# Three buffers for converted weights, a Gram product for the first norm, and seven banks for one projection, in a fused two-block network

## The chip, the cores and the metric

The kernel runs on one core of a Trainium2 chip. The metric is the device time of one launch in microseconds. A core has five engines with their own instruction queues: TensorE (PE), VectorE (DVE), ScalarE (ACT), GpSimd (POOL) and SyncE (SP), which issues transfers. Data lies in HBM, in SBUF (128 partitions) and in PSUM, whose eight banks take PE's sums.

## The reference, cut to what matters

One sequence of 512 tokens of width 1024 passes through a first block and then through two hybrid layers (gqa, mLSTM, neighbourhood and differential attention, gated up projections, an FFN). The first block:

```python
xn = rmsnorm(x, norm1_w[l])
p = xn @ w_in[l]
z, xbc, dt_raw, p_rwkv, p_hgrn, p_gate = jnp.split(p, in_splits, axis=-1)
y_ssm = ssd_branch(z, xbc, dt_raw, ...) @ w_branch_ssm[l]
y_rwkv = rwkv7_branch(p_rwkv, ...) @ w_branch_rwkv[l]
y_hgrn = hgrn2_branch(p_hgrn, ...) @ w_branch_hgrn[l]
gates = jax.nn.sigmoid(p_gate).reshape(b, L, N_BRANCH, D_MODEL)
mixed = gates[:, :, 0] * y_ssm + gates[:, :, 1] * y_rwkv + gates[:, :, 2] * y_hgrn
x = x + mixed @ w_out[l]
h_gate, h_up = jnp.split(rmsnorm(x, norm2_w[l]) @ ffn_w_in[l], 2, axis=-1)
x = x + (jax.nn.silu(h_gate) * h_up) @ ffn_w_down[l]
```

`rmsnorm` divides by the root of the mean square over the 1024 channels; `ssd_branch` ends in such a norm too. All of it is f32.

## The kernel before, in words

Activations lie with channels on partitions and tokens along the row, as tiles of 128x512. A product of f32 quality is made of three f16 products: operands are split into a high and a low part, and xh·whi, xl·whi and xh·wlo are summed in PSUM (L1181 to L1183 in `fm_g`; L1216 to L1218 where the weight is the moving side).

**Weights.** They stream from HBM in units of 128x1024 (512 KB). `_emit_unit` puts one into a staging tile (`wst` for the foreground stream, `bst` for the background stream, two buffers each), ScalarE makes the high part (`whi`/`bhi`, L1070) and VectorE the low part (`wlo`/`blo`, L1071). Every second background unit of the early stages goes another way (L1065 to L1067, with GpSimd). One plain unit feeds 24 products. `take` hands out the next unit and, ahead of that, converts as many further units as `_room` allows: with two buffers per tag, one unit in use and one to come. `self.tags` counts the buffers that are taken.

**The FFN** (`ffn`, once per block or layer, 22 pairs of gate and up tiles) has, for every third pair, a product in seven parts of half width instead of eight ("sevenths", `seventh`, L1424 to L1426), whose weights are sums of quarters: `_emit_seventh` forms them with VectorE (`bw`, L1106, L1110), splits them (L1119 ScalarE or its mirror, L1120 VectorE) and puts them into whichever of the four weight tags is least used. Between products VectorE combines partial sums and scales them (L1440), GpSimd multiplies gate and up (POOL, L1440), and ScalarE and VectorE split the result into `hh` and `hl` (L1231, L1235). PE's outputs turn over five `acc` banks and two background banks bg0 and bg1 (`bank`).

**The first block.** `start` loads x (eight tiles), splits it into xh and xl, and calls `square_sums` for each: ScalarE squares (L1248), VectorE adds (L1250, into `sqa`), and PE sums over partitions by products with a column of ones (L1254). `rms` and `rows_of` turn the sums into a row `rb` over tokens (L1307 to L1309). After that the recurrent scans run, mixed with gates and projections that wait for no scan. At the end the state space branch (`ssd`) gives ysh and ysl and its own norm row `rbs`, and `up` makes the three up projections wbr, wbh and wbs in background mode: for each of eight outputs it loads a gate (`ug`, two buffers), for wbs multiplies it by rbs (L1336), lets PE make 24 products into bg0 or bg1 in turn, multiplies (L1341, L1343) and adds into `mg` on GpSimd (L1345). `out_ffn` then splits mg into mh and ml for the output projection wo1, whose every unit needs all eight.

**Order.** The program is written out by Python generators; a scheduler of the tile framework then sets each engine's order and its waits, so a change of one buffer count shifts rows through the whole program.

Of the kernel before, what the change touches and what calls it, by code (L numbers as in the profile page):

```python
# [11 lines left out]
F16 = mybir.dt.float16  # L12
# [13 lines left out]
PS = 1024.0  # L26
EPS = 1e-6
UB = 8
H = T // 2
FF7 = tuple(range(1, NF, 3))  # L30

# [203 lines left out]
class First:  # L235
# [686 lines left out]
    def first(self, next_gain):  # L922
        parts = lambda p, n, k: (self.t(p, [128, k, T], n + "h", F16), self.t(p, [128, k, T], n + "l", F16))
        pool = self.tc.tile_pool
        if True:
            gd = self.t(self.dram, [24, 128, T], "gd", bufs=1)
            yd = self.t(self.dram, [2, 2, 128, 4, T], "yd", F16, 1)
            with self.banks(acc=1, S=2, T=1, O=1, H=1), pool(name="f_rwkv", bufs=1) as mid, pool(name="f_rwkvs", bufs=2) as small:
                self.mid, self.small = mid, small
                gates, hgrn, due = self.gates("w1", 14, 24, gd), self.hgrn(yd[1]), [0.0, 0.0]  # L930

                def beside(g, h):
                    for n, (more, lane) in enumerate(((gates, 1), (hgrn, 0))):
                        due[n] += (g, h)[n]
                        self.lane, self.bgmode = lane, n == 1
                        while due[n] >= 1:
                            due[n] -= 1
                            next(more, None)
                    self.lane, self.bgmode = None, False

                self.rwkv(yd[0], beside)
                beside(1000, 1000)
            with ExitStack() as mgs:
                mp = mgs.enter_context(pool(name="f_mg", bufs=1))
                self.mg = self.t(mp, [128, 8, T], "mg")
                self.keep2 = self.upp = mp
                ysm = parts(mp, "ys", 8)
                yr, yg = parts(mp, "yr", 4), parts(mp, "yg", 4)
                with self.banks(acc=1, S=2, T=1, O=2), pool(name="f_ssd", bufs=1) as mid, pool(name="f_ssds", bufs=2) as small:
                    self.mid, self.small = mid, small  # L950
                    rbs = self.ssd(*ysm)
                    for y, d in ((yr, yd[0]), (yg, yd[1])):
                        for n in range(2):
                            self.nc.sync.dma_start(out=y[n], in_=d[n])
                    self.background(
                        self.up(gd, 1, "wbr", *yr, 4, True),
                        self.up(gd, 2, "wbh", *yg, 4),
                        self.up(gd, 0, "wbs", *ysm, 8, False, rbs),
                    )
                self.spare = False  # L960
                self.out_ffn(mgs, "wo1", "n2_f", "wf1", "wd1", "fin1", "x", next_gain, ("win0", 46))


class Net(First):
    def __init__(self, ctx, tc, io, cols_at, rows_at, order=None):
# [31 lines left out]
        self.known = order is not None  # L997
        self.emitted, self.taken, self.ready = [0, 0], [0, 0], {}
        self.bgmode, self.dense, self.spare, self.turn = False, False, True, 0
        self.lane, self.other = None, 1  # L1000


    def nm(self, s):
# [43 lines left out]
    def bank(self):  # L1047

        self.turn += 1
        n = self.nb["acc"]  # L1050
        if self.lane is not None or self.bgmode or (self.dense and self.turn % (n + 2) >= n):
            self.other = 1 - self.other if self.lane is None else self.lane
            return self.t(self.bgp, [128, T], f"bg{self.other}", bufs=1)
        return self.b("acc")


    def _emit_unit(self, s, name, u):
# [1 line left out]
        tag = "wb"[s]  # L1059
        st = self.t(self.wst, [128, UB, 128], tag + "st", F32, 2)  # L1060
        nc.sync.dma_start(out=st, in_=self.io[name][u])
        hi = self.t(self.wsp, [128, UB, 128], tag + "hi", F16, 2)
        lo = self.t(self.wsp, [128, UB, 128], tag + "lo", F16, 2)
        if s and self.spare and self.emitted[1] % 2:
            nc.scalar.activation(out=st, in_=st, func=AF.Copy, scale=WS)  # L1065
            nc.scalar.copy(out=hi, in_=st)
# [25 lines left out]
    def _emit_seventh(self, e, name, u, m):  # L1092
# [20 lines left out]
        if m == 6:  # L1113
            del self.staged[name, u]
        tag = min(("bhi", "blo", "whi", "wlo"), key=lambda t: self.tags[t])
        o = self.t(self.wsp, [128, 2, 4, 128], tag, F16, 2)
        self.tags[tag] += 1
        hi, lo = o[:, 0, 0:n], o[:, 1, 0:n]
        nc.scalar.activation(out=hi, in_=src, func=AF.Copy, scale=WS)  # L1119
# [3 lines left out]
    def _room(self, s, e, i):  # L1123
# [3 lines left out]
            return True  # L1127
        if s:
            at = lambda n: n[-1] if n[:2] == "wi" or n[:3] == "wup" else "f"
            return e < i + 2 and at(name) == at(self.items[s][i][0])  # L1130
        if m is None:
            plain = sum(k is None for _, _, k in self.items[s][i:e + 1])
            return plain < 3 and all(self.tags[t] < 2 for t in ("whi", "wlo"))
        return self.opened and min(self.tags.values()) < 2

    def take(self, name, u, m=None):
        s = int(self.bgmode)
# [132 lines left out]
    def rms(self, n, scale, within=None):  # L1270
# [3 lines left out]
        nc.vector.tensor_reduce(out=s, in_=self.ssq[:, 8 * n:8 * n + 8].rearrange("p (t k) -> p t k", k=2), axis=AX.X, op=ALU.add)  # L1274
        if within is not None:
            nc.vector.tensor_tensor(out=s, in0=s, in1=within, op=ALU.mult)
        f = 1.0 / (scale * scale)
        nc.vector.tensor_scalar(out=s, in0=s, scalar1=f / D, scalar2=f * EPS, op0=ALU.mult, op1=ALU.add)
        r = self.t(self.norms, [128, 4], f"rt{n}")
# [106 lines left out]
    def start(self, gain):  # L1386
        nc = self.nc
        with self.banks(acc=5, T=1), self.tc.tile_pool(name="x_in", bufs=1) as p:
            self.sqp = p
            x = self.t(p, [128, 8, T], "x")  # L1390
            for k in range(0, 8, 2):
                (nc.sync if k % 4 else nc.scalar).dma_start(out=x[:, k:k + 2], in_=self.xd[:, k:k + 2])
            for k in range(8):
                self.norm_tile(k, x[:, k], gain)
            self.norm_end()

    def out_ffn(self, mg, wout, gain2, wff, wdn, gain, last=False, after=None, then=None):

# [764 lines left out]
```

## Time and profile before

| | before |
|---|---|
| median of 3 runs | 3617.13 us (3607.03 to 3620.99) |
| profiled execution | 3613.31 us |
| its span, first to last instruction | 3611.6 us |
| mean granted PE clock | 0.976 |
| PE busy | 3338.2 us, 92% |
| VectorE busy | 2760.1 us, 76% |
| ScalarE busy | 1608.3 us, 45% |
| GpSimd busy | 752.6 us, 21% |

Stages by the profile's time: scans to about 680 us, the state space branch and the up projections to 1010, the first FFN's products from about 1080 to 1440, a hybrid layer to 2130, its FFN to 2540, the second layer to 3200, its FFN to the end. A wait that the profile puts beside a PE instruction is time in which PE stood idle just before it, with what ended that time.

### The profile page before, as it was taken

The page shows a single profiled execution, that of the slowest core. Times are in us where ns is not written, and L with a number is a line of the kernel's source. Part 1 is how long each engine was busy: PE and PEld are TensorE (multiplying, and loading weights), DVE is VectorE, ACT ScalarE, POOL GpSimd, SP SyncE. Part 2 cuts the span into 40 slices and gives each one's busy share as a digit, 9 for nine tenths or more (in the row PEclk, how much of TensorE's full clock was granted, in tenths as well). Part 3 has the DMA queues.
Part 4 walks back from the last instruction along what each step waited for, and adds up shares of the span by engine and source line. Part 5 has one row for each costly group of instructions (what it writes and reads, how often), then busy time and mean ns, then how long its engine had stood idle before and what let it go on. Part 6 is the DMA issues. An engine that isn't in the chain of part 4 may idle for free. (4 is left out here: it accounts for less than half of the span.)

```text
span 3611.6 us, 60781 instructions
## 1 busy us (share of the span) xinstructions
PE 3338.2 (92%) x23758; PEld 2033.9 (56%) x23758; DVE 2760.1 (76%) x5599; ACT 1608.3 (45%) x3009; POOL 752.6 (21%) x782
## 2 busy tenths in 40 slices
PE   7899999899899999999989999999999989999998
PEld 3565566555455577556545545568655545545567
DVE  6877777587777798788767677788788767777788
ACT  4232333255344344464556543344364455534443
POOL 2222223223332211201221132211201120132211
PEclk9999999899899999999999999999999999999999
DMA  4312213233242234323223353335322323363333
GB/s 141 82 57 59 75 49 91 72 126 114 88 164 94 94 106 146 106 63 96 93 82 109 116 159 96 96 112 159 111 65 80 94 90 100 112 185 110 94 100 94
DMA packets 151156, 368.16 MB, mean 102 GB/s; under 512 B 44098, under 2 KB 47428, under 8 KB 150868
## 3 DMA queue, kind: packets, MB, share of 16 engines
q1 hardware_dynamic: 117492, 336.03, 30.0%
q0 software_dynamic: 7680, 23.00, 1.9%
q10 hardware_dynamic: 25696, 5.25, 0.8%
q8 instruction: 186, 3.05, 0.4%
q14 instruction: 102, 0.84, 0.1%
HBM read 322.72 MB, written 40.04 MB: 100 GB/s over the span
## 5 line engine op out<-in xcount | busy, mean ns | idle before, releaser
L1181 PE MATMUL acc<-xh,whi 128*128 128x512 f16 x1224 | 469.5, 384 | 28.3 <-DVE g L1706 7.5
L1183 PE MATMUL acc<-xh,wlo 128*128 128x512 f16 x1224 | 469.0, 383 | 23.7 <-DVE wlo L1071 23.6
L1182 PE MATMUL acc<-xl,whi 128*128 128x512 f16 x1224 | 468.9, 383 | 0.0
L1070 ACT ACTIVATE whi<-wst 128x1024 f16<-128x1024 f32 x264 | 275.3, 1049 | 310.3 <-PE acc L1182 147.1
L1071 DVE SCALAR_TENSOR_TENSOR wlo<-wst,whi 128x1024 f16<-128x1024 f32 x264 | 353.9, 1341 | 15.9 <-ACT whi L1070 14.3
L1183 PEld LDWEIGHTS <-wlo 128*128 128x128 f16 x1824 | 179.6, 98 | 257.3 <-DVE wlo L1071 51.4
L1182 PEld LDWEIGHTS <-whi 128*128 128x128 f16 x1824 | 179.9, 99 | 226.6 <-issue 41.9
L1181 PEld LDWEIGHTS <-whi 128*128 128x128 f16 x1824 | 180.6, 99 | 210.4 <-issue 12.4
L1183 PE MATMUL bg<-xh,blo 128*128 128x512 f16 x596 | 230.9, 387 | 3.4 <-DVE reset L309 3.2
L1181 PE MATMUL bg<-xh,bhi 128*128 128x512 f16 x596 | 230.9, 387 | 0.4 <-DVE hk L810 0.4
L1182 PE MATMUL bg<-xl,bhi 128*128 128x512 f16 x596 | 230.6, 387 | 0.0
L1440 POOL TENSOR_TENSOR w<-w,w 128x512 f32<-128x512 f32 x66 | 117.5, 1780 | 448.4 <-DVE w L1440 282.1
L1216 PE MATMUL acc<-whi,xh 128*128 128x128 f16 x1152 | 195.1, 219 | 3.1 <-DVE xp L1758 1.3
L1218 PE MATMUL acc<-whi,xl 128*128 128x128 f16 x1152 | 195.0, 219 | 0.0
L1217 PE MATMUL acc<-wlo,xh 128*128 128x128 f16 x1152 | 195.0, 219 | 0.0
L1070 ACT ACTIVATE bhi<-bst 128x1024 f16<-128x1024 f32 (+1 forms) x132 | 121.7, 934 | 129.4 <-PE bg L1182 89.7
L1071 DVE SCALAR_TENSOR_TENSOR blo<-bst,bhi 128x1024 f16<-128x1024 f32 (+1 forms) x132 | 160.8, 1223 | 13.7 <-ACT bhi L1070 12.1
L1183 PE MATMUL bg<-xh,wlo 128*128 128x512 f16 x408 | 157.3, 386 | 9.1 <-DVE wlo L1071 9.1
L1181 PE MATMUL bg<-xh,whi 128*128 128x512 f16 x408 | 157.4, 386 | 3.0 <-ACT whi L1070 1.8
L1182 PEld LDWEIGHTS <-bhi 128*128 128x128 f16 x980 | 97.6, 100 | 109.0 <-issue 20.1
L1183 PEld LDWEIGHTS <-blo 128*128 128x128 f16 x980 | 97.5, 100 | 106.9 <-issue 6.8
L1181 PEld LDWEIGHTS <-bhi 128*128 128x128 f16 x980 | 97.9, 100 | 105.4 <-issue 9.8
(666 smaller groups left out, 9256.9 us busy)
## 6 DMA issues: line engine op xcount, KB each, us to landing
wst<-win SPq DMA_DIRECT2D x92, 512.0 KB, 3.6
bst<-win SPq DMA_DIRECT2D x64, 512.0 KB, 3.7
wst<-wff SPq DMA_DIRECT2D x60, 512.0 KB, 3.5
wst<-w SPq DMA_DIRECT2D x58, 512.0 KB, 3.6
gd<-bw SPq DMA_DIRECT2D x88, 256.0 KB, 2.2
ug<-gd SPq DMA_DIRECT2D x88, 256.0 KB, 2.7
wst<-wf SPq DMA_DIRECT2D x30, 512.0 KB, 3.5
bst<-w SPq DMA_DIRECT2D x20, 512.0 KB, 3.6
```

Of the source, the lines that this page charges most:

```text
L1070: nc.scalar.activation(out=hi[:, h], in_=st[:, h], func=AF.Copy, scale=WS)
L1071: nc.vector.scalar_tensor_tensor(out=lo[:, h], in0=st[:, h], scalar=WS, in1=hi[:, h], op0=ALU.mult, op1=ALU.subtract)
L1181: mm(ps, lhsT=wh, rhs=h[:, k, :], start=(k == 0), stop=False)
L1182: mm(ps, lhsT=wh, rhs=l[:, k, :], start=False, stop=False)
L1183: mm(ps, lhsT=wl, rhs=h[:, k, :], start=False, stop=(k == nk - 1))
L1216: mm(o, lhsT=xh, rhs=wh, start=(k == 0), stop=False)
L1217: mm(o, lhsT=xh, rhs=wl, start=False, stop=False)
L1218: mm(o, lhsT=xl, rhs=wh, start=False, stop=(k == 7))
L1440: tt = lambda eng, o, x, y, op=ALU.add: eng.tensor_tensor(out=o, in0=x, in1=y, op=op)
```

## The change

Three edits. The tiles `whi`, `wlo`, `bhi` and `blo` have three buffers instead of two (`WB`), and the limits in `_room` are raised to fit: two units to come instead of one, and twelve slots for sevenths instead of eight. Staging keeps two buffers. The wbs projection takes its banks in the order bg, O, S, bg, O, S, acc. And in `start` PE multiplies each of x's 128x128 blocks, in f32, with itself (32 products into four banks); VectorE takes the diagonal by a product with the identity and sums it, four times, instead of ScalarE's squares and VectorE's adds. `rms` is cut in two so that its second half, `inverse`, can be called alone.

```diff
+WB = 3
@@ first
-                        self.up(gd, 0, "wbs", *ysm, 8, False, rbs),
                     )
+                    self.wide = (None, "O", "S", None, "O", "S", "acc")
+                    self.background(self.up(gd, 0, "wbs", *ysm, 8, False, rbs))
+                    self.wide = None
@@ bank
         n = self.nb["acc"]
+        if self.wide:
+            self.turn2 += 1
+            tag = self.wide[self.turn2 % len(self.wide)]
+            if tag:
+                return self.b(tag)
@@ _emit_unit
-        hi = self.t(self.wsp, [128, UB, 128], tag + "hi", F16, 2)
-        lo = self.t(self.wsp, [128, UB, 128], tag + "lo", F16, 2)
+        hi = self.t(self.wsp, [128, UB, 128], tag + "hi", F16, WB)
+        lo = self.t(self.wsp, [128, UB, 128], tag + "lo", F16, WB)
@@ _emit_seventh
-        o = self.t(self.wsp, [128, 2, 4, 128], tag, F16, 2)
+        o = self.t(self.wsp, [128, 2, 4, 128], tag, F16, WB)
@@ _room
-            return e < i + 2 and at(name) == at(self.items[s][i][0])
+            return e < i + WB and at(name) == at(self.items[s][i][0])
-            return plain < 3 and all(self.tags[t] < 2 for t in ("whi", "wlo"))
-        return self.opened and min(self.tags.values()) < 2
+            return plain <= WB and all(self.tags[t] < WB for t in ("whi", "wlo"))
+        return self.opened and min(self.tags.values()) < WB
@@ start
+            gram = [self.b("acc")[:, 0:128] for _ in range(4)]
             for k in range(8):
-                self.norm_tile(k, x[:, k], gain)
-            self.norm_end()
+                self.split(self.xh[:, k, :], self.xl[:, k, :], x[:, k], self.col(gain, k))
+                for i in range(4):
+                    xi = x[:, k, 128 * i:128 * i + 128]
+                    nc.tensor.matmul(gram[i], lhsT=xi, rhs=xi, start=(k == 0), stop=(k == 7))
+            s = self.t(self.norms, [128, 4], "ssq", bufs=2)
+            for i in range(4):
+                junk = self.w(128)
+                nc.vector.tensor_tensor(out=junk, in0=gram[i], in1=self.ident, op=ALU.mult)
+                nc.vector.tensor_reduce(out=s[:, i:i + 1], in_=junk, axis=AX.X, op=ALU.add)
+            self.rt = self.inverse(0, s, IWS)
```

In the three places below, line numbers of the changed kernel are higher by 8 to 24: L1071 has become L1079, L1440 L1464, L1235 L1243, L1370 L1383, L1181 to L1183 L1189 to L1191.

VectorE in the first FFN, at a seventh pair's combinations (L1440), before; `wlo` is a plain unit's low part:

```order
L1440 TENSOR_TENSOR w_1684_10133<-acc_1690_10171,w_1681_10130 128x256
L1235 SCALAR_TENSOR_TENSOR hl_1608_9721<-tt_1680_10123,hh_1607_9720 128x1024
L1440 TENSOR_TENSOR w_1681_10130<-acc_1688_10155,w_1684_10133 128x256
L1440 TENSOR_TENSOR w_1684_10133<-bg0_1691_10186,w_1684_10133 128x256
L1071 SCALAR_TENSOR_TENSOR wlo_1695_10205<-wst_1693_10202,whi_1694_10204 128x1024
L1440 TENSOR_TENSOR w_1683_10132<-acc_1688_10155,w_1684_10133 128x256
L1440 TENSOR_TENSOR w_1683_10132<-bg1_1692_10201,w_1684_10133 128x256
L1440 TENSOR_TENSOR w_1681_10130<-acc_1696_10221,w_1681_10130 128x256
L1071 SCALAR_TENSOR_TENSOR wlo_1700_10239<-wst_1698_10236,whi_1699_10238 128x1024
```

The same place in the changed kernel:

```order
L1079 SCALAR_TENSOR_TENSOR wlo_1690_10164<-wst_1688_10161,whi_1689_10163 128x1024
L1243 SCALAR_TENSOR_TENSOR hl_1619_9765<-w_1681_10141,hh_1618_9764 128x512
L1383 TENSOR_TENSOR tt_1682_10149<-w_1681_10141,tt_1682_10149 128x256
L1383 TENSOR_TENSOR tt_1682_10149<-w_1681_10141,w_1673_10071 128x256
L1383 TENSOR_TENSOR tt_1682_10149<-w_1681_10141,tt_1682_10149 128x256
L1464 TENSOR_TENSOR w_1686_10159<-acc_1692_10193,w_1683_10156 128x256
L1243 SCALAR_TENSOR_TENSOR hl_1619_9765<-tt_1682_10149,hh_1618_9764 128x1024
L1464 TENSOR_TENSOR w_1683_10156<-acc_1691_10180,w_1686_10159 128x256
L1464 TENSOR_TENSOR w_1686_10159<-bg1_1693_10208,w_1686_10159 128x256
L1464 TENSOR_TENSOR w_1685_10158<-acc_1691_10180,w_1686_10159 128x256
L1464 TENSOR_TENSOR w_1685_10158<-bg0_1694_10223,w_1686_10159 128x256
L1079 SCALAR_TENSOR_TENSOR wlo_1698_10241<-wst_1696_10238,whi_1697_10240 128x1024
```

The first unit after the sevenths, converted inside the combinations before, now stands ahead of them; the second stands where the first stood, one operation later.

PE in the last up projection wbs, around the sum over ysh's squares (L770, ones and sqa) and the row of it (L1308), before:

```order
L1181 MATMUL bg0_1501_9022<-ysh_1095_6729,bhi_1496_8982 128x512
L1181 LDWEIGHTS bhi_1503_9025
L1181 MATMUL bg1_1506_9059<-ysh_1095_6729,bhi_1503_9025 128x512
L770 MATMUL T_1436_8668<-ones_81,sqa_1156_7117 128x1 x4
L1182 LDWEIGHTS bhi_1496_8982
L1182 MATMUL bg0_1501_9022<-ysl_1096_6730,bhi_1496_8982 128x512
```

And after:

```order
L1189 MATMUL O_1511_9089<-ysh_1100_6758,bhi_1501_9012 128x512
L1189 LDWEIGHTS bhi_1494_8970
L1189 MATMUL bg0_1506_9051<-ysh_1100_6758,bhi_1494_8970 128x512
L771 MATMUL T_1441_8697<-ones_81,sqa_1161_7146 128x1 x4
L1190 LDWEIGHTS bhi_1501_9012
L1190 MATMUL O_1511_9089<-ysl_1101_6759,bhi_1501_9012 128x512
```

The first two outputs, open at that point, lay in bg0 and bg1; they lie in bg0 and O, and a third, in S, is open too. Behind the row of sums PE had 1 product left on open outputs and then began the next one in bg0; it now has 22 left, on O and S, and then begins the next one in bg1.

VectorE in the scan stage of the first block, before (L361 and L530 are steps of two scans):

```order
L361 TENSOR_TENSOR bon_1586<-fv_1436,acc_1584 128x512
L530 COPY uv_115_571<-S_1602 64x128
L866 TENSOR_TENSOR hr_744<-hr_744,hp_742 128x2x4x64
L1071 SCALAR_TENSOR_TENSOR wlo_1928<-wst_1925,whi_1927 128x1024
L544 TENSOR_TENSOR z_1612<-z_1400,S_1609 128x256
```

And after:

```order
L531 COPY uv_117_593<-S_1691 64x128
L847 TENSOR_TENSOR hw_1894<-hq_685,hp_772 128x2x4x64
L848 TENSOR_TENSOR hw_1895<-hk_773,hr_774 128x2x4x64
L1079 SCALAR_TENSOR_TENSOR wlo_1958<-wst_1955,whi_1957 128x1024
L545 TENSOR_TENSOR z_1701<-z_1642,S_1698 128x256
```

In both a conversion stands between a copy of uv and the step z behind it. Before it is the 23rd conversion of the program; after, one step of that scan later, it is the 24th, of the next unit. The 23rd of the changed kernel stands 29 rows ahead of it.

## Rows read from the trace of the kernel before

**Rows 1.** The page's first part: busy us, share of the span, instructions.
```profile
PE 3338.2 (92%) x23758; PEld 2033.9 (56%) x23758; DVE 2760.1 (76%) x5599; ACT 1608.3 (45%) x3009; POOL 752.6 (21%) x782
```

**Rows 2.** Waits of PE, whole span: line, releaser, us in total, times, longest.
```profile
PE acc L1183 <- DVE wlo L1071: 23.6, 26, 1.9
...
PE bg L1183 <- DVE wlo L1071: 9.1, 7, 1.8
...
PE acc L1426 <- DVE whi L1120: 8.2, 12, 1.4
...
PE bg L1426 <- DVE whi L1120: 8.0, 9, 1.1
...
PE acc L1181 <- ACT whi L1070: 5.5, 8, 0.7
```

**Rows 3.** Waits of PE from 30 to 680 us, the scans.
```profile
PE bg L1216 <- DVE hi L816: 9.9, 2, 6.2
...
PE acc L1183 <- DVE wlo L1071: 1.9, 1, 1.9
```

**Rows 4.** Windows, first FFN: PE, PEld, DVE, ACT, POOL busy, PEclk, DMA.
```profile
1080.00:1340.00 260.00, 245.79 (x1574) 152.13 (x1573) 210.38 (x347) 112.95 (x177) 48.62 (x29) 1.00 0.31 99
```

**Rows 5.** Timeline of VectorE in the first FFN: start, us, what [idle before].
```profile
1139.43 1.21 DVE L1440 TENSOR_TENSOR w<-acc,w 128x256 f32<-128x256 f32 x3
1140.55 1.22 DVE L1071 SCALAR_TENSOR_TENSOR wlo<-wst,whi 128x1024 f16<-128x1024 f32 x1
```

**Rows 6.** Timeline of PE at the same place.
```profile
1140.88 0.38 PE L1182 MATMUL bg<-xl,whi 128*128 128x512 f16 x1
1141.82 0.39 PE L1183 MATMUL bg<-xh,wlo 128*128 128x512 f16 x1 [0.57 <-DVE wlo L1071]
1142.05 0.38 PE L1181 MATMUL bg<-xh,whi 128*128 128x512 f16 x1
```

**Rows 7.** The page's groups: busy us, mean ns of one, idle before and releaser.
```profile
L1070 ACT ACTIVATE whi<-wst 128x1024 f16<-128x1024 f32 x264 | 275.3, 1049 | 310.3 <-PE acc L1182 147.1
L1071 DVE SCALAR_TENSOR_TENSOR wlo<-wst,whi 128x1024 f16<-128x1024 f32 x264 | 353.9, 1341 | 15.9 <-ACT whi L1070 14.3
```

**Rows 8.** Waits of PE from 940 to 1010 us, the projection wbs.
```profile
PE bg L1181 <- DVE ug L1341: 4.1, 1, 4.1
PE bg L1181 <- DVE ug L1343: 3.7, 1, 3.7
PE bg L1181 <- ACT ysh L1231: 2.7, 1, 2.7
```

**Rows 9.** Timeline of PE in wbs.
```profile
978.40 0.59 PE L1181 MATMUL bg<-ysh,bhi 128*128 128x512 f16 x1 [4.07 <-DVE ug L1341]
...
983.90 0.54 PE L1182 MATMUL bg<-ysl,bhi 128*128 128x512 f16 x1
```

**Rows 10.** Timeline of PE at the start.
```profile
17.34 1.87 PE L1254 MATMUL T<-ones,sqa 128*128 128x1 f32 x8 [17.34 <-DVE sqa L1250]
...
24.98 0.61 PE L1183 MATMUL bg<-xh,blo 128*128 128x512 f16 x1 [3.19 <-DVE reset L309]
```

**Rows 11.** Timeline of ScalarE at the start: x's third tile.
```profile
10.12 0.72 ACT L1231 ACTIVATE xh<-x,cols 128x512 f16<-128x512 f32 x1 [1.41 <-DMA x<-xT]
```

**Rows 12.** Timeline of PE: f32 products of 128x128, at the full pace.
```profile
30.59 1.05 PE L1308 MATMUL T<-w,ones 128*128 128x128 f32 x8
```

**Rows 13.** Timeline of VectorE at the start.
```profile
20.95 0.17 DVE L1274 TENSOR_REDUCE ssq<-T 128x4 f32<-128x8 f32 x1 [3.00 <-PE T L1254]
...
24.30 3.15 DVE L1071 SCALAR_TENSOR_TENSOR blo<-bst,bhi 128x512 f16<-128x512 f32 x2
```

**Rows 14.** Waits of ScalarE from 1080 to 1440 us; its timeline at 1138 us.
```profile
ACT hh L1231 <- POOL w L1440: 40.0, 17, 3.5
...
1138.64 0.42 ACT L1231 ACTIVATE hh<-w 128x256 f16<-128x256 f32 x1 [2.58 <-POOL w L1440]
1138.96 1.99 ACT L1070 ACTIVATE whi<-wst 128x1024 f16<-128x1024 f32 x2
```

More of the change, by code (lines that the diff above doesn't have):

```diff
@@ L999, in __init__ @@
         self.bgmode, self.dense, self.spare, self.turn = False, False, True, 0
-        self.lane, self.other = None, 1
+        self.lane, self.other, self.wide, self.turn2 = None, 1, None, -1
     def nm(self, s):
@@ L1276, in rms, with inverse @@
             nc.vector.tensor_tensor(out=s, in0=s, in1=within, op=ALU.mult)
+        return self.inverse(n, s, scale)
+    def inverse(self, n, s, scale):
+        nc = self.nc
         f = 1.0 / (scale * scale)
@@ L1392, in start @@
                 (nc.sync if k % 4 else nc.scalar).dma_start(out=x[:, k:k + 2], in_=self.xd[:, k:k + 2])
+            gram = [self.b("acc")[:, 0:128] for _ in range(4)]
             for k in range(8):
-                self.norm_tile(k, x[:, k], gain)
-            self.norm_end()
+                self.split(self.xh[:, k, :], self.xl[:, k, :], x[:, k], self.col(gain, k))
[8 more added lines that the diff above has]
+            self.rt = self.inverse(0, s, IWS)
+            self.rb = self.t(self.norms, [128, T], "rb")
+            self.rows_of(self.rt, self.rb)
     def out_ffn(self, mg, wout, gain2, wff, wdn, gain, last=False, after=None, then=None):
```

## The prediction

> **What bounds the kernel now.** I read the share of busy time first. TensorE (PE) works 92% of the span [rows 1], so time can only go where PE stands still or runs at its lower clock. Next came the waits of PE over the whole span, sorted by what ended them [rows 2]. Beside waits inside the scans and the attention, five rows of one kind stand near the top: PE waits for a converted weight, the low part (wlo, by VectorE) or the high part (whi, by ScalarE or VectorE). They sum to 23.6 + 9.1 + 8.2 + 8.0 + 5.5 = 54.4 us in 62 waits, none over 1.9 us. The same view of the scan stage [rows 3] has only 1.9 us of it; there VectorE's own chain (hi, 9.9 us in two waits) is what PE waits for. So 52.5 us lie outside the scan, nearly all in the three feed forward nets (FFN).
>
> Is VectorE then simply too slow there? The windows [rows 4] say no: in the first FFN it is busy 210.38 of 260 us (81%), PE 245.79. The average has room, the moment has not. One place shows it: VectorE's combination of a seventh's partial products runs from 1139.43, the conversion behind it from 1140.55 [rows 5], and PE, which issued its last product on that unit's high part at 1140.88, stands 0.57 us before it gets the low part at 1141.82 [rows 6]. A unit feeds PE 24 products at 0.22 us a start (1141.82 to 1142.05 in [rows 6]), 5.2 us; converting it costs ScalarE 1049 ns and VectorE 1341 ns [rows 7]. With two buffers a conversion that falls behind a cluster of other work has one unit's time to recover.
>
> **Part 1, three buffers.** It removes and adds no instruction; it moves conversions one unit ahead. In the FFN (order fences of the change) a conversion that stood inside the combinations now stands ahead of them. One more plain unit is 5.2 us of cover; for the sevenths, whose slots go from 8 to 12, four more of some 1.3 us each (12 products of half the width, so half of 0.22) are as much. The longest wait was 1.9 us, so cover alone would take all 52.5 us. I take four fifths, 42 us: several conversions in a row can be late where ScalarE or VectorE is held up (rival 1), and VectorE's 19% of free time has to pay off any such debt. Ends: all, 52.5, and half, 26.
>
> In the scans and attention the order shows the spots of conversions within a scan step of where they were, each holding the next unit's conversion instead. A scan step has the same number of conversions ahead of it between neighbours, and only at a stage's start is one more done, 1.3 us of VectorE [rows 7]; I book 0, between +4 (one at the start of each of the three mixed stages, nothing beside it) and -1.9 [rows 3]. The staging buffers stay at two and are freed one unit sooner, so their transfers only start sooner.
>
> **Part 2, seven banks.** In the last up projection PE waits 3.7 us and 4.1 us for VectorE to empty one of two banks [rows 8]. The second, ending at 978.40, is followed by 13 products at the slow pace, from 978.40 to 983.90 [rows 9], 0.42 us a start against 0.22. In the new order the outputs go to bg0, O, S, bg1, O, S, acc, and 22 products on banks O and S stand where PE waited for ug. So 4.1 us go. Of the 3.7 I take 1.5: soon after it PE waits for ysh (2.7 us) [rows 8], the end of the state space chain, which banks don't hasten; arriving there earlier only lengthens that wait. Of the slow stretch (13 x 0.20 = 2.6 us lost) I take 1.4. Sum 7. Ends: 10.4 (everything), and -1, a loss, if the drains, which keep VectorE's order, set the end and the output projection wo1, which needs all eight outputs for its first unit, starts no sooner.
>
> The Trainium skill, page "TensorE: Matmul & The Clock Gate", section "HAM oscillation — how this bites in real kernels", speaks against this part: for a kernel that loops its contraction without a break, more PSUM buffering gave no further gain. By that rule this term would be 0 and the sum 7 us smaller. The wait of 4.1 us in [rows 8] is for a bank, so I go by the row.
>
> **Part 3, x's sums of squares.** Gone are 8 Squares on ScalarE, 6 adds on VectorE, and PE's 16 records of width 1 at the start. Added are 32 products of 128x128 in f32 and 8 small VectorE operations. PE starts at 17.34 now [rows 10]; it will start when x lands. The third tile is there at 10.12 [rows 11], so 24 products remain. A product of this kind costs up to 1.05/4 = 0.26 us at the full pace [rows 12]; for the lower pace the nearest row has 1.87/4 = 0.47 us [rows 10]. The sums end between 10.1 + 24 x 0.26 = 16.4 and 10.1 + 24 x 0.47 = 21.4. Now they end at 20.9, where VectorE takes them over [rows 13]. Behind that on VectorE stand, before and after, two wlo conversions (1341 ns each [rows 7]) and the first blo, at 24.30 [rows 13], and PE can't pass its third product without blo: 24.98 [rows 10], 4.1 us after the sums. Eight small operations of 0.17 us, as the one at 20.95 [rows 13], make it 5.5 us. So blo comes at 21.9 to 26.9 against 24.98: -3.1 to +1.9. PE's products from 24.98 on come at the slow pace (0.61 us long [rows 10], 0.38 in [rows 6]); with 0.2 us lost in each of some eight, up to 1.6 us can come back, an estimate. I take -1.5, ends -4.7 and +1.9.
>
> **Sum.** 42 + 7 + 1.5 = 50.5 us off the profiled execution's 3613.3: 3562.8. The median of the runs stands 3.8 us above that execution, so 3566.6.
>
> **Rivals.**
> Half: VectorE, at 81%, catches up between clusters only in part; FFN 26, rest 8.5, together 34.5: 3582.6. For it: 61 separate waits show that it is late regularly. Against: its idle time is real.
> Rival 1, it doesn't do what it says: the conversion is late by its place in an engine's order, not for want of a buffer. ScalarE's hh waits 40.0 us for GpSimd's product in the first FFN, and at the place above two whi start only at 1138.96, behind a hh that had waited 2.58 us [rows 14]. Then a third buffer is filled as late as the second, and only 8.5 us go: 3608.6. Against: most whi conversions wait for PE, 147.1 us in all [rows 7], which is a wait for a free buffer. The Trainium skill, same page, section "Architectural detail: the array is 16× 32×32, not 1× 128×128", says that ScalarE and VectorE take their work strictly in order; that is the mechanism of this rival.
> Rival 2, slower: the conversions that now stand ahead of the combinations hold up the release of accumulators, and PE waits for these instead. There are 33 waits for wlo in [rows 2]; with one conversion of 1.34 us [rows 7] at each, and the old waits not gone, +44 - 8.5 = +36: 3653. It beats the other 8.5 us from 0.26 us a place, and passes 0.5% from 0.8 us. Against it: before, no row of [rows 2] has PE waiting for a combination, with seven banks to turn over.
>
> **How the numbers follow.** Forecast 0.60, half 0.20, rival 1 0.13, rival 2 0.07. I predict 3566. The range runs from all ends together on the good side (52.5 + 10.4 + 4.7 + 1.9 = 69.5 off, 3547.6, and 5 us for the shuffled order) to just short of rival 1, 3606; rivals 1 and 2 are the 0.2 left out. A measurement tells about 0.5%, 18 us, from no change, so faster means under 3599: forecast and half, less a little for the reach of the latter's end, 0.77; same 0.16; slower 0.07.
>
> **What would show it.** Right: the five rows of [rows 2] fall from 54 to about 11 us; the wait for ug at 978 is gone; PE's first instruction starts near 6 to 7 us and the first blo product before 25. Part 1 is wrong if the wlo rows stay above 25 us, or a row with PE waiting for the combinations appears. Part 2 is wrong if the output projection starts no sooner after the state space norm than before. The whole is wrong if the mixed stages, whose spots I read as unchanged, differ by over 15 us.

## The result and the profile after

| | before | after |
|---|---|---|
| median of 4 runs | 3612.26 us (3607.03 to 3620.99) | 3567.84 us (3564.7 to 3572.34) |
| profiled execution | 3613.31 us | 3568.91 us |
| PE busy | 3338.2 us, 92% | 3344.1 us, 94% |
| mean granted PE clock | 0.976 | 0.974 |

The ratio is 0.9876, with a 95% interval from 0.985 to 0.9902: 44 us less. PE stands idle for 50.3 us less of the span and is busy for 5.9 us more: it has 48 more records, and in this execution it spends 189 us at the lower granted clock instead of 172. The page's first part and the two groups that answer to [rows 1] and [rows 7]:

```profile
PE 3344.1 (94%) x23806; PEld 2055.0 (58%) x23806; DVE 2736.6 (77%) x5600; ACT 1602.6 (45%) x3001; POOL 771.2 (22%) x782
...
L1078 ACT ACTIVATE whi<-wst 128x1024 f16<-128x1024 f32 x264 | 276.7, 1051 | 327.8 <-PE acc L1190 164.6
L1079 DVE SCALAR_TENSOR_TENSOR wlo<-wst,whi 128x1024 f16<-128x1024 f32 x264 | 329.6, 1249 | 32.3 <-ACT whi L1078 30.9
```

The waits of PE over the whole span (line, releaser, us in total, times, longest). Of the five rows of [rows 2] one is left, with 1.0 us. All the rows in which PE waits for a converted weight (whi, wlo, bhi, blo) add up to 8.0 us, against 63.8 before; the largest is now a seventh's (4.6 us), and the top of the list is something else:

```profile
PE acc L1189 <- DVE w L757: 18.0, 7, 4.8
PE T L1262 <- POOL sqa L1258: 12.8, 5, 5.3
...
PE acc L1450 <- DVE bhi L1128: 4.6, 4, 1.7
...
PE acc L1448 <- ACT bhi L1127: 1.2, 3, 0.4
...
PE acc L1450 <- DVE whi L1128: 1.0, 1, 1.0
...
PE bg L1191 <- DVE blo L1079: 0.7, 1, 0.7
...
PE acc L1450 <- DVE blo L1128: 0.5, 1, 0.5
```

The waits for sqa were 4.4 us before; two of them, 5.3 and 4.6 us, now stand between the first two FFNs and the layers behind them, within the hybrid layers' rows of the table below.

Windows of the first FFN's products, first of the kernel before and then of after (start:end, length, busy us of PE, PEld, VectorE, ScalarE, GpSimd, granted clock). PE's idle time goes from 12.6 us to 0.8 us (over the three FFNs from 44.2 to 4.8), beside a VectorE as busy as before (78% and 80%):

```profile
1071.00:1293.00 222.00, 209.41 (x1241) 119.88 (x1240) 172.57 (x280) 90.59 (x136) 46.16 (x28) 1.00 0.30 96
```

```profile
1075.00:1282.00 207.00, 206.25 (x1236) 120.77 (x1235) 166.16 (x277) 88.75 (x135) 53.46 (x28) 1.00 0.33 103
```

Stage by stage, from the times in the two traces at which PE first uses an operand. "Scans" runs from the first product on xh to the first on the state space branch's wdh, "state space" from the first on yr to the first on ysh, "wbs" from there to the output projection wo1, "FFN" from an output projection's last product to the first product of the down projection (hh).

| stage | before | after | change |
|---|---|---|---|
| start, to the first product on xh | 20.8 | 17.9 | -2.8 |
| scans | 681.1 | 682.7 | +1.6 |
| state space | 233.1 | 244.2 | +11.1 |
| wbs | 75.4 | 65.6 | -9.8 |
| FFN 1, 2, 3 | 238.8, 245.4, 243.2 | 227.4, 227.8, 229.0 | -11.4, -17.6, -14.2 |
| down projections, first to last product on hh | 109.1, 105.4, 103.4 | 109.7, 105.1, 103.3 | +0.6, -0.3, -0.1 |
| hybrid layers, from there to their output projection | 704.5, 704.9 | 706.4, 701.6 | +1.9, -3.3 |

The FFNs give 43.2 us; wbs and the start give 12.6, and the state space stage takes 11.1 of that back. With the scans' 1.6 nothing is left of it: the output projection wo1, whose operand is mh, begins at 1013.3 us in both kernels. First the kernel before, then after (first and last start in the fourth place):

```profile
L1181 PE MATMUL acc<-mh,whi x144: 376/379/379, 1013.3 to 3248.6; 128*128 128x512 f16 x144
```

```profile
L1189 PE MATMUL acc<-mh,whi x144: 377/379/379, 1013.3 to 3218.4; 128*128 128x512 f16 x144
```

So all of the 44 us arise behind that point, in the FFNs and what stands beside them.

### The profile page after: what moved, and what is told of

Its sections match the earlier page's. It is cut to its first block, busy times and chain, and to the rows that moved or that the text cites. A ratio compares the mean times of both kernels' runs of the same rounds, so it can differ in the third digit from the quotient of the medians.

```text
span 3567.2 us, 60900 instructions
## 1 busy us (share of the span) xinstructions
PE 3344.1 (94%) x23806; PEld 2055.0 (58%) x23806; DVE 2736.6 (77%) x5600; ACT 1602.6 (45%) x3001; POOL 771.2 (22%) x782
## 4 chain that ended last, share of the span: by engine, by line
PE 44%; DVE 31%; issue 8%; ACT 7%; POOL 5%; DMA 4%; ACTq 0%; SPq 0%; DVEq 0%; POOLq 0%
PE bg L1190 4%; PE bg L1191 4%; PE bg L1189 4%; PE acc L1189 3%; PE acc L1190 3%; PE acc L1191 3%; DVE wlo L1079 3%; POOL w L1464 2%; DVE bw L1118 2%; DVE w L1464 2%; PE acc L1224 1%; PE acc L1450 1%; PE acc L1449 1%; PE acc L1448 1%; PE acc L1226 1%
## 5 line engine op out<-in xcount | busy, mean ns | idle before, releaser
L1189 PE MATMUL acc<-xh,whi 128*128 128x512 f16 x1224 | 472.2, 386 | 34.5 <-DVE w L757 18.0
L1191 PE MATMUL acc<-xh,wlo 128*128 128x512 f16 x1224 | 471.2, 385 | 0.0
L1078 ACT ACTIVATE whi<-wst 128x1024 f16<-128x1024 f32 x264 | 276.7, 1051 | 327.8 <-PE acc L1190 164.6
L1079 DVE SCALAR_TENSOR_TENSOR wlo<-wst,whi 128x1024 f16<-128x1024 f32 x264 | 329.6, 1249 | 32.3 <-ACT whi L1078 30.9
L1191 PEld LDWEIGHTS <-wlo 128*128 128x128 f16 x1824 | 180.3, 99 | 210.8 <-issue 15.3
L1189 PEld LDWEIGHTS <-whi 128*128 128x128 f16 x1824 | 181.3, 99 | 200.3 <-issue 11.3
L1189 PE MATMUL bg<-xh,bhi 128*128 128x512 f16 x596 | 230.1, 386 | 5.8 <-DVE hk L811 5.7
L1191 PE MATMUL bg<-xh,blo 128*128 128x512 f16 x596 | 229.8, 386 | 4.5 <-DVE reset L310 4.5
L1464 POOL TENSOR_TENSOR w<-w,w 128x512 f32<-128x512 f32 x66 | 121.8, 1846 | 403.9 <-DVE w L1464 331.8
L1079 DVE SCALAR_TENSOR_TENSOR blo<-bst,bhi 128x1024 f16<-128x1024 f32 (+1 forms) x132 | 155.5, 1182 | 6.8 <-ACT bhi L1078 5.8
L1189 PE MATMUL bg<-xh,whi 128*128 128x512 f16 x408 | 158.1, 387 | 0.5 <-ACT bw L1334 0.5
L1190 PE MATMUL bg<-xl,whi 128*128 128x512 f16 x408 | 157.9, 387 | 0.0
L1191 PE MATMUL bg<-xh,wlo 128*128 128x512 f16 x408 | 157.7, 386 | 0.0
L1190 PEld LDWEIGHTS <-bhi 128*128 128x128 f16 x980 | 97.2, 99 | 105.0 <-issue 15.5
L1191 PEld LDWEIGHTS <-blo 128*128 128x128 f16 x980 | 96.8, 99 | 103.1 <-issue 7.1
```

Source lines behind the costliest of these rows:

```text
L1078: nc.scalar.activation(out=hi[:, h], in_=st[:, h], func=AF.Copy, scale=WS)
L1079: nc.vector.scalar_tensor_tensor(out=lo[:, h], in0=st[:, h], scalar=WS, in1=hi[:, h], op0=ALU.mult, op1=ALU.subtract)
L1189: mm(ps, lhsT=wh, rhs=h[:, k, :], start=(k == 0), stop=False)
L1190: mm(ps, lhsT=wh, rhs=l[:, k, :], start=False, stop=False)
L1191: mm(ps, lhsT=wl, rhs=h[:, k, :], start=False, stop=(k == nk - 1))
L1464: tt = lambda eng, o, x, y, op=ALU.add: eng.tensor_tensor(out=o, in0=x, in1=y, op=op)
```

## The experiments

Each kernel's stages, taken from its trace as above. "FFN" is the sum of the three, "slow" the time within the scans at the lower granted clock.

| kernel | median us | scans (slow) | state space | wbs | FFN |
|---|---|---|---|---|---|
| before | 3612.3 | 681.1 (76) | 233.1 | 75.4 | 727.4 |
| after | 3567.8 | 682.7 (85) | 244.2 | 65.6 | 684.2 |
| e1: parts 2 and 3 alone | 3596.9 | 675.2 (65) | 234.5 | 72.0 | 723.7 |
| e2: part 1 alone | 3566.6 | 672.5 (62) | 243.1 | 71.5 | 679.9 |
| e3: after, without seven banks | 3565.5 | 681.9 (88) | 241.8 | 71.5 | 682.2 |
| e4: part 3 alone | 3599.2 | 679.5 (76) | 234.5 | 73.7 | 722.6 |
| e5: raised limits in the FFN only | 3574.6 | 689.3 (92) | 243.7 | 65.6 | 683.9 |
| e6: background one unit ahead | 3554.7 | 668.7 (72) | 244.1 | 65.6 | 681.7 |
| e7: eight slots for sevenths | 3568.9 | 671.8 (67) | 241.6 | 65.6 | 689.2 |
| e8: e1 with three staging buffers | 3597.6 | 704.3 (122) | 236.5 | 72.1 | 699.7 |
| e9: whi, wlo three; bhi, blo two | 3564.4 | 690.4 (121) | 235.4 | 71.9 | 680.0 |
| e10: whi, wlo two; bhi, blo three | 3597.6 | 690.9 (108) | 245.2 | 65.6 | 719.2 |
| e11: after, again | 3561.8 | 683.4 (93) | 240.0 | 65.5 | 681.4 |
| e12: e6, again | 3559.2 | 678.5 (89) | 243.5 | 65.6 | 683.3 |

### The parts, one by one

e1 has the Gram sums and the seven banks without the buffers:

```diff
-WB = 3
+WB = 2
```

> The changed kernel with two converted buffers per tag again (the limits with them), so the Gram sums and the seven banks alone. Theory (the buffers carry the gain): the three FFNs' products take as long as in the kernel before, about 223, 229 and 227 us from the first xsh product to the first hh product, the five weight waits stay at about 50 us, and the time is 8 to 13 us under the kernel before. Rival (the gain comes from the shuffled order): FFNs shorter by over 5 us each without the third buffer. The state space stage lost 11 us in the changed kernel (703.6 to 947.8 us against 704.9 to 938.0): if the third buffer did that, this kernel takes about 233 us there, if the seven banks did it, about 244.

Measured 0.9964 of the kernel before (0.9951 to 0.9977), 13 us. The FFNs keep all but 4 of their 727 us, and the state space stage is at 234.5: neither the FFNs' gain nor the longer state space stage is the seven banks' or the Gram sums' doing.

e2 is the kernel before with the edits of `_emit_unit`, `_emit_seventh` and `_room` alone.

> The kernel before with three converted buffers and the raised limits, nothing else. Theory: FFNs at 209, 211 and 210 us as in the changed kernel, 43 us less in all, start and wbs as before; 30 to 45 us under the kernel before, the less the more of the state space stage's 11 us the buffers cause. Rival: the third buffer is filled as late as the second, and the time is within 10 us of the kernel before.

Measured 0.9889 (0.9865 to 0.9912), 44 us: the whole of the change's gain by itself. FFNs 47.5 us shorter, state space stage 10 us longer. Beside the buffers, parts 2 and 3 show no gain in the whole time (3566.6 us here, 3567.8 for the change). The theory holds; its rival, that a third buffer fills as late as the second, is out.

e3 takes the seven banks out of the changed kernel:

```diff
-                    )
-                    self.wide = (None, "O", "S", None, "O", "S", "acc")
-                    self.background(self.up(gd, 0, "wbs", *ysm, 8, False, rbs))
-                    self.wide = None
+                        self.up(gd, 0, "wbs", *ysm, 8, False, rbs),
+                    )
```

> The changed kernel with the state space up projection on bg0 and bg1 again. Theory: the segment from the first ysh product to the output projection returns from 65.6 to about 75 us, and the wait for ug of about 4 us is back. If the seven banks also caused the longer state space stage ahead of it (244 us), that stage returns to about 233 and the total stays as it is, within 5 us of the changed kernel; if not, the total is about 10 us above the changed kernel.

Measured 0.9862 (0.9842 to 0.9881), no slower than the changed kernel. One of its four executions took 16941 us and is left out of this ratio; the median of the other three is 3563.5 us. By the stages the banks still give 5.9 us in wbs (71.5 to 65.6), and they aren't what lengthened the state space stage (241.8). So 3.9 us of wbs's 9.8 come with the third buffer, not with the banks. I had expected 75 us, and a wait for ug of about 4 us; it is 2.8 us, as in e2. The whole time doesn't show the 5.9 us: neither of the two cases that I had spelled out came.

e4 takes both the buffers and the banks out (e1 with e3's edit), which leaves the Gram sums.

> The kernel before with the Gram sums alone. Theory: the first product on xh starts at about 18 us instead of 20.8, the first on a low part (blo) at 22 to 24 instead of 25; the lead is 3 us or less by the end of the scans, and the time within 5 us of the kernel before. Rival: the lead is lost in the scans altogether, since these wait for their own chain on VectorE; then 0.

Measured 0.9973 (0.9962 to 0.9983), 11 us, more than either theory. The first product on xh starts at 16.5 us, 4.3 us sooner, and small differences of 1.6 to 4.8 us in the scans, wbs, the first hybrid layer and the FFNs add up to the rest. That part is not explained by the start; the parts' sum over the program (e1 13 and e2 44) is also 11 to 13 us more than the change as a whole gives (44), so figures of this size per part can't be added.

### Which limit, and which buffer

e5 keeps three buffers everywhere but lets `take` run two units ahead only in `out_ffn`:

```diff
-            return e < i + WB and at(name) == at(self.items[s][i][0])
+            return e < i + (WB if self.opened else 2) and at(name) == at(self.items[s][i][0])
-            return plain <= WB and all(self.tags[t] < WB for t in ("whi", "wlo"))
+            n = WB if self.opened else 2
+            return plain <= n and all(self.tags[t] < n for t in ("whi", "wlo"))
```

> The changed kernel with three buffers, but the raised limits hold only within the output projection and the FFN; in the scans, the state space stage and the attention the limits are those of before (two per tag). Theory (the third buffer pays in the FFN and costs in the state space stage): FFN products at about 209, 211 and 210 us, the state space stage from yr to ysh back from 244 to about 234 us, the scans at about 675 us as with two buffers and the Gram sums; 3592 - 46 + about 4 for the start of the projections, so 3545 to 3555 us. Rival (the state space stage's length comes from the scheduler's shuffle and not from the limits there): it stays over 240 us and the time at 3560 to 3570.

Measured 0.991 (0.9891 to 0.9928), 20 to 30 us over what I had expected, and the state space stage stayed at 243.7. My theory on the limits there fell: the code asks for units no earlier than before, and the stage is as long as with the raised limits. What remained was the buffer itself, since the scheduler may place a conversion as soon as a buffer is free; e9 and e10 test that.

e6 lowers the background's limit alone:

```diff
-            return e < i + WB and at(name) == at(self.items[s][i][0])
+            return e < i + 2 and at(name) == at(self.items[s][i][0])
```

> The changed kernel with the background stream's limit back at one unit ahead; the foreground keeps two. It tells which stream's deeper conversion lengthens the state space stage. If the background's (units of wbr, wbh, wbs): yr to ysh about 234 us and 3555 us or less. If the foreground's (units of z): it stays at 242 to 245 us and the time at 3562 to 3570.

Measured 0.9851 (0.9831 to 0.987), state space stage 244.1: with e5, the limit isn't it, on either stream. The time fell to what I had said for the other case, with scans 14 us shorter than the changed kernel's; e12 comes back to that.

e9 and e10 give the third buffer to one stream each, by a count per tag (`WB = {"whi": 3, "wlo": 3, "bhi": 2, "blo": 2}` and its mirror, with the limits per tag). Both have ten slots for the sevenths, so they differ in which plain units have a third buffer.

> The changed kernel with three buffers for whi and wlo (foreground) and two for bhi and blo, the limits with them (ten slots for sevenths). It tells which buffers lengthen the state space stage from about 233 to 244 us. If those of the foreground (z's units come earlier and PE waits in order for z's only accumulator): it stays at 242 to 245 us, with 18 us of waits for w L757. If those of the background: 233 to 236 us. FFNs in both cases within 2 us each of the changed kernel's 209, 211, 210, since plain units use the foreground's buffers.

> The mirror of it: two buffers for whi and wlo, three for bhi and blo. If the plain units' cover carries the gain, the FFNs go back to 220 us or more each (33 of 50 us of waits were theirs), about 3585 to 3595 us. If the state space stage goes with the foreground's buffers, it is at 233 to 236 us here.

Measured 0.986 (0.9843 to 0.9878) and 0.9963 (0.9949 to 0.9977). The two separate cleanly. The foreground's buffers carry the FFN (680.0 against 719.2), as expected. The state space stage goes with the background's (235.4 against 245.2), the other way round from the case that I had spelled out for e10. The table agrees: the five kernels with two background buffers have 233.1 to 236.5 us there, the nine executions with three have 240.0 to 245.2. The waits of PE there, in the kernel before from 700 to 950 us, in e9 from 703 to 970 us and then in e10 over the same window as e9:

```profile
PE acc L1181 <- DVE w L756: 7.1, 6, 2.2
```

```profile
PE acc L1189 <- DVE w L757: 6.5, 6, 1.7
PE bg L1191 <- DVE blo L1079: 6.0, 1, 6.0
```

```profile
PE acc L1189 <- DVE w L757: 16.6, 6, 4.8
PE T L694 <- DVE xs L611: 7.0, 3, 4.4
```

The operation that makes w (L756 before, L757 here) empties the one accumulator that the gate projection z has in that stage. With three background buffers PE waits for it 16.6 to 18 us, with two 6.5 to 7.3 (10.4 in e8). Idle time and slow stretches both grow: by the traces 18.1 us idle and 9.7 us slow before, 23.0 and 21.0 after. The slow part differs between executions of one kernel: the changed kernel again (e11) has 23.3 us idle and 10.0 us slow there and takes 240.0 us, not 244.2. So some 7 of the 11 us come with the third background buffer at an equal slow part. Why it makes PE wait longer is my reading, argued and not shown: the background products of wbr and wbh, converted sooner, have been issued already when z's turn comes, and no longer fill PE's wait for that accumulator. The second row of e9 is the price on the other side: with two background buffers wbs waits 6.0 us once for blo, and takes 71.9 us instead of 65.6.

In e10 the plain units' waits of [rows 2] are back, over the whole span:

```profile
PE acc L1191 <- DVE wlo L1079: 21.1, 13, 2.8
```

e7 gives the sevenths their eight slots again (`min(self.tags.values()) < 2`).

> The changed kernel with eight slots for the sevenths instead of twelve; plain units keep two ahead. The five weight waits of before were 33 us for plain low parts, 16 us for sevenths, 5.5 us for plain high parts. If cover is what counts, each kind by itself, the 16 us of the sevenths come back: each FFN about 5 us longer, 3580 to 3586 us. Rival (the plain units ahead alone free VectorE and ScalarE before the cluster): FFNs stay within 2 us each, and the time within 6 us of the changed kernel.

Measured 0.9884 (0.9866 to 0.9903). By the stages it costs 5.0 us in the FFN column and 6.2 us in the down projections (110.3, 106.5 and 107.5 us), 11 of the 16 us. The stages lean to the theory, the time to the rival: the median is 1 us above the changed kernel's, where the theory had 12 to 18. The traces can't settle it, since the profiled execution of e7 was the fastest of its four (3558.2 us, the others 3568.6 to 3573.1), with scans 11 us shorter than the changed kernel's (below). Nor are the 6.2 us the old waits come back: the kernel before, with eight slots too, spends no longer in its down projections (317.9 us) than the changed kernel (318.1). What twelve slots are worth by themselves stays open.

### Is it the transfer that is late?

e8 is e1 with three staging buffers:

```diff
-        st = self.t(self.wst, [128, UB, 128], tag + "st", F32, 2)
+        st = self.t(self.wst, [128, UB, 128], tag + "st", F32, 3)
-                st = self.t(self.wst, [128, UB, 128], tag, F32, 2)
+                st = self.t(self.wst, [128, UB, 128], tag, F32, 3)
```

> Gram sums and seven banks with two converted buffers, and three staging buffers instead of two, so that a unit's transfer can start earlier. Theory (the converted buffer is what lacked): FFNs as in the kernel before, 223 to 229 us, and the time within 6 us of the kernel with two staging buffers, 3597. Rival (a conversion is late because its data lands late): FFNs shorter by 5 us or more each.

Measured 0.9968 (0.9957 to 0.9979), the time of e1, as the theory had it, but for another reason. The FFNs are 24 us shorter than e1's (6.8, 10.2 and 7.1 us), which is what the rival had said, and the scans, at the lower clock for 122 us, 29 us longer. All seven executions of e8 had a lower mean clock (0.969 to 0.973) than any of e1's (0.977 to 0.979). So the rival was right on the FFNs, for 24 of the 43 us. Waits of ScalarE in the first FFN, where it stands in order behind a seventh's transfer, in the kernel before (1071 to 1293 us) and then in e1 (1059 to 1282 us):

```profile
ACT bhi L1119 <- DMA wst<-wf1s: 15.5, 6, 3.7
```

```profile
ACT hh L1239 <- POOL w L1464: 38.4, 17, 2.8
ACT bhi L1127 <- DMA wst<-wf1s: 16.7, 6, 4.6
```

In e8 the row for wf1s is gone, and PE's waits for a weight there (1093 to 1307 us) are 4.5 us, against 13.4 in e1 (1059 to 1282 us); e8 first, then e1:

```profile
PE acc L1191 <- DVE wlo L1079: 2.7, 4, 0.8
PE bg L1191 <- DVE wlo L1079: 1.5, 2, 0.8
PE acc L1189 <- ACT whi L1078: 0.3, 2, 0.2
```

```profile
PE acc L1191 <- DVE wlo L1079: 7.8, 8, 1.5
PE acc L1189 <- ACT whi L1078: 3.2, 4, 1.2
PE acc L1450 <- DVE whi L1128: 1.2, 2, 0.6
PE bg L1450 <- DVE whi L1128: 0.6, 1, 0.6
PE bg L1191 <- DVE wlo L1079: 0.6, 1, 0.6
```

So part of the lateness was a transfer that began late for want of a staging buffer. In the changed kernel, with two staging buffers, ScalarE's waits for transfers in the same stretch are down to 2.4 us as well. The likely reason is that a conversion that is made one unit sooner frees its staging buffer sooner, so that one added buffer at the end of the line serves both. No run here splits the 43 us between the two, earlier transfers and the cover of a further converted unit.

```profile
ACT whi L1078 <- DMA wst<-wf: 1.9, 2, 1.1
...
ACT bhi L1127 <- DMA wst<-wf1s: 0.5, 1, 0.5
```

### The scans, and the same kernel twice

e7 has the changed kernel's order of PE and VectorE up to the first FFN, and its scans took 671.8 us against 682.7. I ran the changed kernel and e6 again, side by side.

> The changed kernel again, beside the next one. The kernel with eight slots for sevenths has the same order of PE and VectorE up to the first FFN and yet took 671.8 us for the scans against 682.7; the 10 us arose at 150 to 172 us, where four small transfers through DRAM bring G back. If that is how these transfers happen to land, the scans of this profile take anything between 670 and 685 us, and the state space stage, wbs and the FFNs repeat within 2 us each (244, 66, 209, 211, 210).

> The kernel with the background's limit at one unit ahead again, beside the changed kernel on the same chip. If its 13 us lie in the landing of those transfers alone, its time is within 5 us of the changed kernel's and its scans' length varies likewise; if its order in the scans is better, it is 8 to 14 us faster again, with scans of about 669 us.

Measured 0.9865 (0.9846 to 0.9884) and 0.986 (0.9843 to 0.9876). e6's lead of 13 us is 2.6 us when both run on one chip: no version here beats the changed kernel beyond doubt. My cause for the scans' spread, the landing of small transfers, fell: PE's wait for G is 1.9 us in all three. The windows from 150 to 170 us show where the time goes, in the changed kernel and then in e7 (granted clock third from the end):

```profile
150.00:160.00 10.00, 10.00 (x102) 6.70 (x102) 5.29 (x8) 2.71 (x5) 3.02 (x4) 0.56 0.16 48
160.00:170.00 10.00, 10.00 (x85) 5.74 (x84) 2.67 (x5) 1.65 (x5) 0.00 (x0) 0.50 0.02 7
```

```profile
150.00:160.00 10.00, 10.00 (x172) 7.12 (x171) 7.63 (x12) 3.22 (x7) 3.02 (x4) 1.00 0.16 55
160.00:170.00 10.00, 9.89 (x73) 6.94 (x71) 5.75 (x14) 3.84 (x9) 0.00 (x0) 1.00 0.09 20
```

With the same instructions in the same order, PE is granted its lower level (1.2 GHz) for 20.5 us in one execution and the higher one (2.4 GHz) throughout in the other, right after the same short wait and small 32x32 products. That alone is some 10 us. e11 has the same slow stretch of 20.5 us. Why the clock fell in one and not in the other isn't shown. That e7's eight slots aren't needed for it is borne out by the four executions of e11: one kernel on one chip took 3548.2 us at a mean clock of 0.980, and 3561.0, 3562.7 and 3564.3 at 0.975 or 0.976. In e11 wbs and the FFNs repeat as I had expected, but the state space stage doesn't: 240.0 us, where I had said 244 within 2 us.

## Why the prediction was right, point by point

**Time.** 3566 was predicted with a range of 3542 to 3606; 3567.8 came. The sum was 50.5 us off the profiled execution, the traces show 44.4, so it was 6.1 us too much. That the forecast still lies within 2 us is in part luck: I added 3.8 us because the median of three runs stood that far above the profiled execution; with a fourth run it stands 1.1 us below it.

**Part 1 in the FFN, 42 us.** Measured 43.2 (e2 alone 47.5). The five rows that I had seen falling from 54 to about 11 us fell to 1.0. That the foreground's third buffer is the cause is shown by e2, e9 and e10. Cover is not its only way: by e8 a part of the lateness was in the transfers, which I hadn't priced. "Four fifths" was right as a size and wrong in its reason. I spread the loss over all waits; in fact those ahead of the down projections went wholly, and 10.2 us of the 52.5, which lay within the down projections (sevenths waiting for whi: 3.1 + 2.4, 2.0 + 1.0 and 1.7 us in the three of them), brought nothing, since other waits took their place. PE waits 11.3 us in all there before and 11.8 us after, now for sevenths in other buffers and for accumulators (xt, w). The waits of PE in the first down projection, from 1293 to 1403 us before and from 1282 to 1393 us after:

```profile
PE bg L1426 <- DVE whi L1120: 3.1, 3, 1.1
PE acc L1426 <- DVE whi L1120: 2.4, 3, 1.4
PE acc L1426 <- DVE wlo L1120: 1.1, 1, 1.1
```

```profile
PE acc L1450 <- DVE bhi L1128: 2.7, 2, 1.7
PE acc L1448 <- DVE xt L1465: 2.0, 4, 0.9
PE acc L1450 <- DVE whi L1128: 1.0, 1, 1.0
```

Windows of the first down projection, before and then after:

```profile
1293.00:1403.00 110.00, 103.41 (x930) 90.00 (x929) 104.55 (x179) 58.69 (x106) 17.39 (x11) 1.00 0.38 113
```

```profile
1282.00:1393.00 111.00, 104.20 (x932) 90.66 (x931) 106.64 (x179) 58.49 (x107) 19.11 (x11) 1.00 0.38 111
```

VectorE is busy 95% and 96% of it, which leaves it little time to work ahead; that this is why nothing was gained there is argued, not shown (PE is busy 94% too, and in e7 fewer slots cost 6.2 us in the same projections). I had taken the 81% of one window for the whole FFN; the window of [rows 4] reaches from the gate and up products 47 us into the down projection, and mixes 78% with 95%. In the gate and up products PE's waits went, and VectorE had time there.

**Rival 1** (late by its place in the order) fails as a result, by e2, but its picture is true in part: e8 shows that a ScalarE held up by a transfer made weights late. The row that I held against it, whi waiting for PE ([rows 7], 147.1 us), still stands at 164.6 us after: it is ScalarE having time, not a cost, and was no good evidence.

**Mixed stages, 0 (between -1.9 and +4).** This step failed in the state space stage: +11.1 us. I had looked for conversions in VectorE's order within the scans and found them at their old places; I had not looked at what PE does with a background weight that is ready sooner. e9 and e10 show the background's third buffer as its cause; some 4 of the 11.1 us are a slow stretch that e11 doesn't have. The hybrid layers came within 3.3 us of 0, the scans' +1.6 lies within their spread. Together the mixed stages differ by 11.3 us, under the 15 that I had named.

**Part 2, 7 us.** wbs is 9.8 us shorter, near the upper end of 10.4, but only 5.9 of that are the banks' (e3). My own sign for this part holds: from the row of sums over ysh's squares to the first product of wo1 it takes 44.9 us before and 37.8 after (43.4 in e3). The terms were right in what goes, wrong in why. The waits for ug of [rows 8] are 0.7 us after (window 947 to 1014 us):

```profile
PE T L694 <- DVE xs L611: 4.4, 1, 4.4
PE T L771 <- POOL sqa L768: 1.7, 1, 1.7
...
PE bg L1189 <- DVE ug L1356: 0.7, 1, 0.7
```

But with two converted buffers the same banks give only 1.7 us (e4 73.7, e1 72.0), because the wait for a bank turns into one for a weight; e1 from 929 to 1002 us:

```profile
PE bg L1191 <- DVE blo L1079: 6.0, 1, 6.0
PE O L1191 <- DVE blo L1079: 1.5, 1, 1.5
```

The banks are worth 5.9 us only beside the third background buffer, and in that stage only: the whole time shows none of it (e3). What I weighed against this part, that more PSUM buffering gave one kernel no further gain (the Trainium skill, "TensorE: Matmul & The Clock Gate", "HAM oscillation — how this bites in real kernels"), comes near in this stage with two weight buffers and not with three. The end of -1 us, drains that set the end, didn't show.

**Part 3, 1.5 us.** The bounds held at the start; the 11 us of e4, the Gram sums alone, lie outside them, and beside the buffers no gain shows in the whole time. PE at the start, after (each f32 product leaves two records, so x48 is 24 products):

```profile
5.20 3.78 PE L1411 MATMUL acc<-x 128*128 128x128 f32 x16 [5.20 <-DMA x<-xT]
10.51 7.60 PE L1411 MATMUL acc<-x 128*128 128x128 f32 x48 [1.53 <-DMA x<-xT]
...
23.08 0.61 PE L1191 MATMUL bg<-xh,blo 128*128 128x512 f16 x1 [4.54 <-DVE reset L310]
23.48 0.63 PE L1189 MATMUL bg<-xh,bhi 128*128 128x512 f16 x1
```

The sums end at 18.1 (16.4 to 21.4 was said), 24 products in 7.60 us are 0.32 each (0.26 to 0.47), and blo comes at 23.08 against 24.98 (21.9 to 26.9). The slow products behind it stayed slow, 0.40 us a start, so that gift didn't come. PE starts at 5.2 us, sooner than the 6 to 7 that I had said: the first two tiles (8 products) run then, and the rest waits for the third until 10.5.

**Rival 2** (conversions ahead of the combinations hold up accumulators) hardly shows: in the second FFN's gate and up products PE waits 0.8 us for a combination, in the others not at all. In the down projections PE waits 4.4 us for accumulators that VectorE has yet to empty (xt and w, L1465), where before there was no such wait.

**The hit is in part errors that cancel.** The FFNs gave 43.2 us for 42, with the wrong reason for the size. Of the 8.5 us booked for parts 2 and 3 nothing was left at the output projection: start and wbs gave 12.6, the state space stage and the scans, booked at 0, took 12.7 back. The shift of the median hid most of that.

## What to carry to other kernels

Where PE shows many short waits for the same kind of operand while the engines that make it have free time on average, one more buffer at the end of that line can pay, as it did here; give it to the stream that waits, and look at what it does to the others: here the same buffer on the other stream cost some 7 to 11 us elsewhere. More output banks help only as far as operands are there to fill them: try the two together, and look at the whole time as well as at the stage. Before a stage's length is credited to an edit, compare two executions of the same order in that stage, with the granted clock beside them.

## What the runs showed of the hardware that I had not expected

The granted clock in the scans differs between executions of the same order: 20.5 us at the lower level in the changed kernel at 151 us, none in e7, for 10 us of time. Over all kernels here, whose orders differ, the scans took 669 to 704 us with 62 to 122 us at the lower level; the longest had the most of it. Between executions of the same order alone they took 672 to 683 us, a spread as large as parts 2 and 3 together in their stages.
